# Where TensorE's two operands begin in SBUF, modulo 256 bytes, in a one-core hybrid layer

## The chip, the cores and the metric

The kernel runs on one core of one Trainium2 chip. The metric is the device time of one execution in microseconds. Three runs of the kernel before took 1450.31, 1451.68 and 1453.68 us; the median is 1451.68 us.

## The reference

One layer of an encoder trunk on x of 256 frames by 2048 channels, all in float32:

```
mod = silu(c) @ w_ada + b_ada                  # 2048 x 12288, split in six
h = rmsnorm(x, g0) * (1 + sc1) + sh1
q, k, v, r, lr, cb, cc, cx, ga, gb = split(h @ w_in)     # 2048 x 10256
o = gated linear attention(q, k, v, lr), by chunks of 64 frames, 4 heads
y_a = (rmsnorm(o) * silu(r)) @ w_out_gla       # 1024 x 2048
y_b = (cb * conv3(cc * cx)) @ w_out_conv       # 1024 x 2048
y = (sigmoid(ga) * y_a + sigmoid(gb) * y_b) @ w_o        # 2048 x 2048
x = x + g1 * rmsnorm(y, g_1)
h = rmsnorm(x, g_2) * (1 + sc2) + sh2
gate, up = split(h @ w_up)                     # 2048 x 11264
x = x + g2 * rmsnorm((gelu(conv3(gate)) * up) @ w_down, g_3)   # 5632 x 2048
```

## The kernel before

All weights, 362 MB, pass once from HBM through SBUF. Each product a @ w of float32 is made of three float32r matmuls: both operands are split in a rounded part (hi) and the rest (lo), and hi*hi, hi*lo and lo*hi are added up in PSUM. float32r is a 4-byte type that TensorE takes in one pass.

The work is a list, `stream`, of chunks. A chunk (class `Chunk`) is up to two blocks of 128 rows by 512 columns of one weight matrix. `pump` walks over the list: it issues the DMA of a chunk up to 13 places ahead (`LOOK_DMA`) into one of nine `raw` buffers, splits a chunk four places ahead (ScalarE casts `whi`, L283; VectorE subtracts and writes `wlo`, L292), and then has the matmuls of the chunk at hand issued. Between the chunks stand parts of the product with w_ada, which VectorE makes (`Ada` and `Gemv`, L424 to L472).

There are two kinds of matmul groups, and they put the operands the other way round:

- `Feat` (L339): the result has features on the partitions. The weights are stationary (128 columns of `whi` or `wlo`), and the activations move: 256 columns, one per frame, 258 in the first pair of groups of w_up. The activations are `h_hi` and `h_lo` (tile H), `yb` (tag B) for w_out_conv, `og` (tag g8) for w_out_gla, and `xs` (tile H again) for w_up.
- `Tok` (L394): the result has frames on the partitions. 128 frames of an activation are stationary, and 512 columns of the weights move. Stationary are H for k, v0 and v1 of w_in, `m_t` (tile H) for w_o, and `act` (tag g8) for w_down.

Each matmul has one weight load of its own (PEld). The load of the next matmul runs beside the matmul at hand.

All tiles come from one pool, which lays the tags one behind the other in the order of first use. By the allocation of this kernel, the tags that matter begin at these bytes of each partition: B at 31552, g8 at 47936 (four buffers of 8192), H at 85568 (36992 bytes), raw at 123392, whi at 168960, wlo at 185344. Modulo 256, B, all buffers of g8 and H are at 64; raw, whi and wlo are at 0. All steps inside the tiles that a matmul operand makes (a block of 128 or 512 columns, a row of H with 576 columns, 256 frames) are multiples of 256 bytes. So every `Feat` matmul reads its moving activations from 64 and its next stationary weights from 0, modulo 256, and every `Tok` matmul reads its moving weights from 0 and its next stationary activations from 64. The exceptions are small: L694 and L695, the projection for the forget gate, load 32 and 16 columns of a tile `t` that begin at 32 or at 160, beside 256 moving columns of H at 64.

The first stage makes the shift and scale for the first slice of two blocks of 128 channels (`SLICES[0]`). The product with w_ada for it is eight items `Ada(0, 0)` to `Ada(0, 7)`, each of two blocks of 128 rows by 512 columns, with two DMAs of 256 KB. VectorE adds up an item with two instructions (L472) into `acc_s`; the items in `ON_PE` are left to TensorE, which adds them up with small matmuls (L229, `sum_cols`). After the last item VectorE folds `acc_s` (L209, L211), TensorE finishes the sum over partitions (L217, `fold_cols`) into the same PSUM bank, and the first two blocks of H are made (`make_h`); with them the first `Feat` matmul starts.

Of the kernel before, what the change touches and what calls it, by code (L numbers as in the profile page):

```python
# [9 lines left out]
F32R = mybir.dt.float32r  # L10
# [5 lines left out]
P = 128  # L16
T = 256
D = 2048
KD = D // P
H = 4  # L20
# [7 lines left out]
TAU = 16.0  # L28
KT = 2
H_ROW = 576  # L30
NC = 512


# [7 lines left out]
G8 = 4  # L41
# [13 lines left out]
MID0, MID = 2, 4  # L55
SQ0, SQ1 = 3, 4
EARLY_G = [1, 0, 6, 13]
ON_PE = {(0, 5)}


@with_exitstack
def hybrid_layer(ctx, tc, x, c, w_ada, b_ada, norm_g, w_in, w_a2, b_a2, gla_norm_g,
# [7 lines left out]
    def sb(shape, tag, bufs=1, dt=F32):  # L70
        count[0] += 1
        return pool.tile(list(shape), dt, tag=tag, bufs=bufs, name=f"{tag}_{count[0]}")
# [5 lines left out]
    def sm_bank():  # L78
        count[0] += 1
        return psum.tile([P, 512], F32, tag="sm", bufs=2, name=f"sm_{count[0]}")  # L80

    def t2(cols=512):
        return sb([P, cols], "t2", T2)

    def t1(cols=T):
        return sb([P, cols], "t1", T1)
# [67 lines left out]
    def over(row, n):  # L154
        return row.rearrange("p (o t) -> p o t", o=1).to_broadcast([P, n, T])
# [15 lines left out]
    for s in range(2):  # L171
        for q in range(2):
            ps = mm_banks()
            for a in range(8):
                k = 8 * q + a
# [11 lines left out]
    gln = lambda i: p_col[:, 88 + i:89 + i]  # L187


    def moving():  # L190

        t = sb([P, KD * H_ROW + 32], "H", 1, F32R)[:, 0:KD * H_ROW].rearrange("p (k n) -> p k n", k=KD)
        return t[:, :, T:], t[:, :, 0:T]

    h_hi, h_lo = moving()
    mod1 = sb([P, 2, KD], "mod1")
    bmod1 = sb([P, 2, KD], "bmod1")
# [66 lines left out]
    class Chunk:  # L264
# [9 lines left out]
        def dma(self):  # L274
            g = self.g
            self.raw = sb([P, KT, NC], "raw", RAW_BUFS)[:, 0:self.n, :]
            r = g.row0 + self.k0 * P
            nc.sync.dma_start(
                self.raw, g.w[r:r + self.n * P, g.n0:g.n0 + NC].rearrange("(t p) n -> p t n", p=P))

        def split(self):
            self.hi = sb([P, KT, NC], "whi", SPLIT_BUFS, F32R)[:, 0:self.n, :]
            nc.scalar.copy(self.hi, self.raw)  # L283
            self.lo = sb([P, KT, NC], "wlo", SPLIT_BUFS, F32R)[:, 0:self.n, :]
            if pos[2] < first_w:
                first_lo.append(self.split_lo)
            else:
                self.split_lo()
# [154 lines left out]
    class Ada:  # L443
# [17 lines left out]
        def split(self):  # L461
            s = self.s
            for t in range(self.nk):
                if (s, self.i) in ON_PE:
                    break
# [14 lines left out]
        def mm(self):  # L480
            s = self.s
            if (s, self.i) in ON_PE:
                for t in range(self.nk):
# [56 lines left out]
    yb = {}  # L540
# [3 lines left out]
    qk, vt, sr, og = {}, {}, {}, {}  # L544
# [81 lines left out]
    def split_pair(hi, lo, src):  # L626
        copy = nc.scalar.copy(hi, src)
        nc.vector.tensor_sub(lo, src, f(hi))
        return copy.ins

    def tiles(t, n=2):
        return t.rearrange("p (a t) -> p a t", a=n)

    def post_cb(g):
        def post(j, v):
            if not yb:
                yb["t"] = sb([P, 2, 8, T], "B", 1, F32R)
            t = tiles(t2())
            nc.vector.tensor_mul(t, v, cc_t[g][:, 1, j:j + 2, :])
            k = 4 * g + j  # L640
            split_pair(yb["t"][:, 0, k:k + 2, :], yb["t"][:, 1, k:k + 2, :], t)
        return post
# [102 lines left out]
    def keys_values(h):  # L745

        kd = qk["t"][:, 1].rearrange("p (s d) -> p s d", s=2)
        kv = mm_banks()
        for c4 in range(4):
            s, half = c4 // 2, c4 % 2  # L750
            rows = slice(64 * half, 64 * half + 64)
            nc.tensor.matmul(kv[:, half, s * DV:(s + 1) * DV], kd[rows, s, h * DK:(h + 1) * DK],
                             vt["t"][rows, s, h * DV:(h + 1) * DV], start=True, stop=True)
        return kv

    def gla_heads():
        og["hi"] = sb([P, 8, T], "g8", G8, F32R)
        og["lo"] = sb([P, 8, T], "g8", G8, F32R)
        for h in range(H):
            S = sb([P, 4, DV], "c4", 2)  # L760
            kv = kvs.pop(h)
            nc.scalar.copy(S[:, 0, :], kv[:, 0, 0:DV])
            for c4 in range(1, 4):
                nc.vector.scalar_tensor_tensor(
                    S[:, c4, :], S[:, c4 - 1, :], dtot[:, 4 * c4 + h:4 * c4 + h + 1],
                    kv[:, c4 % 2, (c4 // 2) * DV:(c4 // 2 + 1) * DV], op0=ALU.mult, op1=ALU.add)
            yield
            yield
            po = sm_bank()
            qT = qk["t"][:, 0].rearrange("p (h t) -> p h t", h=4)[:, h, :]  # L770
            for dv in range(2):
                for c4 in range(4):
                    nc.tensor.matmul(po[:, dv * T + c4 * 64:dv * T + (c4 + 1) * 64],  # L773
                                     S[:, c4, dv * P:(dv + 1) * P], qT[:, c4 * 64:(c4 + 1) * 64],
                                     start=True, stop=True)
            sq = t2()
            nc.scalar.activation(sq, po, AF.Square)
            yield
            sum2 = t1()
            nc.vector.tensor_add(sum2, sq[:, 0:T], sq[:, T:2 * T])  # L780
            yield
            if h + 1 < H:
                kvs[h + 1] = keys_values(h + 1)
            pm = sm_bank()
            nc.tensor.matmul(pm[:, 0:T], ones, sum2, start=True, stop=True)
            yield
            rs = t1()
            nc.scalar.activation(rs, pm[:, 0:T], AF.Sqrt, scale=1.0 / DV, bias=eps)
            nc.vector.reciprocal(rs, rs)  # L789
            yield  # L790
            o = t2()
            ov = o.rearrange("p (a t) -> p a t", a=2)
            nc.vector.tensor_mul(ov, po.rearrange("p (a t) -> p a t", a=2), over(rs, 2))
            for dv in range(2):
                nc.vector.scalar_tensor_tensor(ov[:, dv, :], ov[:, dv, :], gln(dv), sr["t"][:, 0, 2 * h + dv, :],
                                               op0=ALU.mult, op1=ALU.mult)
            og["last"] = split_pair(og["hi"][:, 2 * h:2 * h + 2, :], og["lo"][:, 2 * h:2 * h + 2, :], ov)
            yield


    m_t, y_t = {}, {}
# [4 lines left out]
    def post_ya(g):  # L806
        def post(j, v):
            if not m_t:
                m_t["hi"], m_t["lo"] = moving()
            k = 4 * g + j  # L810
            t = tiles(t2())
            nc.vector.tensor_mul(t, v, ga_t["t"][:, k:k + 2, :])
            nc.vector.tensor_add(t, t, gb_t["t"][:, k:k + 2, :])
            split_pair(m_t["hi"][:, k:k + 2, 0:T], m_t["lo"][:, k:k + 2, :], t)
        return post
# [299 lines left out]
    run_all(bg)  # L1115

    bg = gla_heads()
    pump(stream.index(gla_to) + 1 - pos[2], each=step_bg)
    run_all(bg)
# [22 lines left out]
    with tc.high_priority():  # L1142
        xs["hi"], xs["lo"] = moving()
        nc.vector.tensor_copy(xs["hi"][:, :, T], sh2)
        nc.vector.tensor_sub(xs["hi"][:, :, T + 1], sh2, f(xs["hi"][:, :, T]))
        for q in range(4):
            n = slice(512 * q, 512 * (q + 1))
            for s in range(2):
                def x1():
                    return nc.vector.scalar_tensor_tensor(  # L1150
                        xin["t"][:, s, n], y_t["t"][:, s, n], r1[:, s:s + 1], xin["t"][:, s, n],
                        op0=ALU.mult, op1=ALU.add).ins
                if len(mid) == 3:
                    with tc.issue_after(mid[2]):
                        x1()
                else:
                    ins = x1()
                    if s == 1:
                        mid.append(ins)
            for k in range(4 * q, 4 * q + 4, 2):  # L1160
                ps = sm_bank()
                for a in range(2):
                    for s in range(2):
                        nc.tensor.transpose(ps[:, a * T + s * P:a * T + (s + 1) * P],  # L1164
                                            xin["t"][:, s, (k + a) * P:(k + a + 1) * P], ident)
                for a in range(2):
                    sc, v = s2[:, k + a:k + a + 1], ps[:, a * T:(a + 1) * T]
                    hi = xs["hi"][:, k + a, 0:T]
                    mid_act.append(nc.scalar.mul(hi, v, sc).ins)
                    nc.vector.scalar_tensor_tensor(xs["lo"][:, k + a, :], v, sc, f(hi),  # L1170
                                                   op0=ALU.mult, op1=ALU.subtract)
# [63 lines left out]
```

## Time and profile before

| | us |
|---|---|
| median of the runs shown | 1451.68 |
| the profiled execution's own time | 1453.29 |
| span of its trace, first to last instruction | 1451.5 |
| TensorE matmuls busy (PE) | 1425.8 (98%) |
| weight loads busy (PEld) | 1336.3 (92%) |
| VectorE busy (DVE) | 1036.6 (71%) |
| ScalarE busy (ACT) | 792.9 (55%) |

The span stands beside the execution's own time: 1.8 us lie around it. A matmul's duration in the trace runs from its start to the end of its drain, so it overlaps with the next ones; what counts for the time is the distance from one start to the next, which a row of the chain of waits gives as its time divided by its count.

### The profile page before, as it was taken

Reading aid. Unit: us, or ns where it says so; the run is one execution under the profiler, and the core shown is the slowest. Engines: PE = TensorE matmul, PEld = TensorE weight load, DVE = VectorE, ACT = ScalarE, POOL = GpSimd, SP = SyncE. Lnnn points to the kernel's source line nnn. Section 1 sums busy time; section 2 is a strip of 40 time slices with the busy share of each in tenths; the row PEclk is TensorE's granted clock in tenths of the full one; section 3 lists DMA queues with packets and bytes.
Section 4 is the critical chain, followed back from the end, with each engine's and each line's share of the span. In section 5 each row is a group of like instructions: output and inputs, shape, how many; then the busy total and the mean of one; then the engine's idle time right before and its main releaser. Section 6 shows DMA issues by size and latency. Waiting matters only on the chain.

```text
span 1451.5 us, 25558 instructions
## 1 busy us (share of the span) xinstructions
PE 1425.8 (98%) x10385; PEld 1336.3 (92%) x10385; DVE 1036.6 (71%) x1153; ACT 792.9 (55%) x952; POOL 7.1 (0%) x28
## 2 busy tenths in 40 slices
PE   6999999999999999999999999999999999999997
PEld 6999999899999999887999998789999988999986
DVE  6887878889988877975897666656666644555554
ACT  5788777689554655444764444344444433444443
POOL 0000000000000000000000000000000000000000
PEclk9999999999999999999999999999999999999999
DMA  9999989989988778886568777677776666666651
GB/s 353 366 339 310 375 286 360 328 288 331 372 285 280 245 251 317 304 299 183 151 199 264 238 234 235 231 239 236 230 228 204 200 188 190 187 184 185 186 174 59
DMA packets 178095, 366.97 MB, mean 253 GB/s; under 512 B 14026, under 2 KB 26648, under 8 KB 177209
## 3 DMA queue, kind: packets, MB, share of 16 engines
q1 hardware_dynamic: 176857, 362.17, 75.4%
q0 software_dynamic: 544, 2.11, 0.4%
q8 instruction: 81, 1.33, 0.4%
q10 hardware_dynamic: 576, 1.05, 0.2%
q14 instruction: 37, 0.30, 0.1%
HBM read 363.18 MB, written 2.11 MB: 252 GB/s over the span
## 4 chain that ended last, share of the span: by engine, by line
PE 93%; DVE 3%; DMA 2%; ACT 1%; issue 1%; SPq 0%; DVEq 0%; ACTq 0%
PE mm L339 63%; PE mm L394 28%; DMA raw<-in_w_ada_dram 2%; DMA XF<-in_x_dram 1%; DVE wlo L292 0%; DVE c L432 0%; DMA raw<-in_w_in_dram 0%; PE sm L1164 0%; SPq L458 0%; ACT whi L283 0%; DVE t L789 0%; PE sm L773 0%; DVE fold L211 0%; DVE c L472 0%; PE sm L217 0%
## 5 line engine op out<-in xcount | busy, mean ns | idle before, releaser
L283 ACT CAST whi<-raw 128x1024 fp32r<-128x1024 f32 (+1 forms) x503 | 512.6, 1024 | 525.3 <-PE mm L339 280.4
L292 DVE TENSOR_TENSOR wlo<-raw,whi 128x1024 fp32r<-128x1024 f32 (+1 forms) x503 | 595.4, 1191 | 285.5 <-ACT whi L283 275.7
L339 PE MATMUL mm<-H,whi 128*128 128x256 f32 (+1 forms) x4992 | 649.3, 281 | 1.6 <-ACT H L254 1.2
L339 PEld LDWEIGHTS mm<-H,whi 128*128 128x128 f32 x4992 | 616.1, 189 | 3.9 <-ACT H L254 1.3
L339 PE MATMUL mm<-H,wlo 128*128 128x256 f32 (+1 forms) x2496 | 350.2, 280 | 0.0
L339 PEld LDWEIGHTS mm<-H,wlo 128*128 128x128 f32 x2496 | 318.5, 188 | 0.0
L394 PE MATMUL mm<-whi,g 128*128 128x512 f32 x704 | 181.5, 395 | 0.0
L394 PEld LDWEIGHTS mm<-whi,g 128*128 128x128 f32 x704 | 131.9, 188 | 31.7
L432 DVE SCALAR_TENSOR_TENSOR c<-raw,sil,c 128x1024 f32<-128x1024 f32 x90 | 115.2, 1280 | 35.7 <-DMA raw<-in_w_ada_dram 35.6
L394 PE MATMUL mm<-whi,H 128*128 128x512 f32 x448 | 118.5, 396 | 0.0
L394 PEld LDWEIGHTS mm<-whi,H 128*128 128x128 f32 x448 | 83.5, 188 | 19.6
L394 PE MATMUL mm<-wlo,g 128*128 128x512 f32 x352 | 99.3, 395 | 0.0
L394 PEld LDWEIGHTS mm<-wlo,g 128*128 128x128 f32 x352 | 66.1, 188 | 16.0
L472 DVE SCALAR_TENSOR_TENSOR c<-raw,sil,c 128x768 f32<-128x768 f32 (+2 forms) x73 | 78.6, 1077 | 2.0 <-DMA raw<-in_w_ada_dram 1.4
L394 PE MATMUL mm<-wlo,H 128*128 128x512 f32 x224 | 65.7, 395 | 0.0
L432 DVE SCALAR_TENSOR_TENSOR cb<-raw,sil,cb 128x1024 f32<-128x1024 f32 x30 | 38.5, 1284 | 24.7 <-DMA raw<-in_w_ada_dram 24.7
L394 PEld LDWEIGHTS mm<-wlo,H 128*128 128x128 f32 x224 | 42.1, 188 | 10.2
L982 DVE SCALAR_TENSOR_TENSOR t<-mm,fcol,t 128x255 f32<-128x255 f32 x80 | 38.4, 480 | 1.2
L339 PE MATMUL mm<-B,whi 128*128 128x256 f32 x256 | 33.5, 282 | 0.0
L339 PE MATMUL mm<-g,whi 128*128 128x256 f32 x256 | 32.8, 280 | 0.0
L339 PEld LDWEIGHTS mm<-B,whi 128*128 128x128 f32 x256 | 31.4, 188 | 1.4 <-ACT t L712 0.8
L339 PEld LDWEIGHTS mm<-g,whi 128*128 128x128 f32 x256 | 31.3, 188 | 0.0
(193 smaller groups left out, 687.1 us busy)
## 6 DMA issues: line engine op xcount, KB each, us to landing
raw<-in_w_up_dram SPq DMA_DIRECT2D x176, 512.0 KB, 4.3
raw<-in_w_ada_dram SPq DMA_DIRECT2D x160, 512.0 KB, 5.2
raw<-in_w_in_dram SPq DMA_DIRECT2D x145, 512.0 KB, 5.8
raw<-in_w_down_dram SPq DMA_DIRECT2D x88, 512.0 KB, 3.8
raw<-in_w_o_dram SPq DMA_DIRECT2D x32, 512.0 KB, 5.6
raw<-in_w_ada_dram SPq DMA_DIRECT2D x32, 384.0 KB, 6.1
raw<-in_w_out_conv_dram SPq DMA_DIRECT2D x16, 512.0 KB, 6.1
raw<-in_w_out_gla_dram SPq DMA_DIRECT2D x16, 512.0 KB, 5.4
```

The lines of the kernel that those rows point to most:

```text
L283: nc.scalar.copy(self.hi, self.raw)
L292: nc.vector.tensor_sub(self.lo, self.raw, f(self.hi))
L339: nc.tensor.matmul(dst[:, 0:cols], w[:, t, j * P:(j + 1) * P], m(ch.k0 + t, cols), start=first_in_bank and t == 0 and i == 0, stop=end and ...
L394: nc.tensor.matmul(self.out[s], m(c.k0 + t, T)[:, s * P:(s + 1) * P], w[:, t, :], start=first and t == 0 and i == 0, stop=end and t == c.n ...
L432: nc.vector.scalar_tensor_tensor(a, self.raw, sil[:, self.k:self.k + 1], a, op0=ALU.mult, op1=ALU.add)
L472: nc.vector.scalar_tensor_tensor(a, raw, sc, a, op0=ALU.mult, op1=ALU.add)
L982: nc.vector.scalar_tensor_tensor(dst[:, a, i:], v[:, a, 0:T - i], w(2 - i, a), dst[:, a, i:], op0=ALU.mult, op1=ALU.add)
```

## The change

Three things are done.

- A tile for moving activations gets 64 more elements, and the activations begin 32 elements (`OPPOSITE`, 128 bytes) inside it: H where it is `h` and `xs`, `yb`, and both parts of `og`. H has 48 elements (`H_PAD`) behind its rows instead of 32. Where H holds `m_t`, the stationary activations of w_o, it begins at the tile's beginning, as `act` does in its unchanged tile.
- Since B grows by 256 bytes, each of the four buffers of g8 by 256, and H by 64, all tiles behind H (raw, c4, whi, wlo, A, cb and the small ones) move up by 1344 bytes, which is 64 modulo 256. The tiles ahead of them keep their places modulo 256.
- `ON_PE` names the last item of the first slice, (0, 7), in place of (0, 5).

```diff
+H_PAD = 48
+OPPOSITE = 32
-ON_PE = {(0, 5)}
+ON_PE = {(0, 7)}
-    def moving():
-        t = sb([P, KD * H_ROW + 32], "H", 1, F32R)[:, 0:KD * H_ROW].rearrange("p (k n) -> p k n", k=KD)
+    def parted(shape, tag, bufs=1):
+        n = shape[0] * shape[1]
+        t = sb([P, n + 64], tag, bufs, F32R)[:, OPPOSITE:OPPOSITE + n]
+        return t.rearrange("p (k n) -> p k n", k=shape[0])
+    def moving(at=OPPOSITE):
+        t = sb([P, KD * H_ROW + H_PAD], "H", 1, F32R)[:, at:at + KD * H_ROW]
+        t = t.rearrange("p (k n) -> p k n", k=KD)
         return t[:, :, T:], t[:, :, 0:T]
-                yb["t"] = sb([P, 2, 8, T], "B", 1, F32R)
+                yb["t"] = parted([16, T], "B").rearrange("p (a k) n -> p a k n", a=2)
-        og["hi"] = sb([P, 8, T], "g8", G8, F32R)
-        og["lo"] = sb([P, 8, T], "g8", G8, F32R)
+        og["hi"] = parted([8, T], "g8", G8)
+        og["lo"] = parted([8, T], "g8", G8)
-                m_t["hi"], m_t["lo"] = moving()
+                m_t["hi"], m_t["lo"] = moving(0)
```

## Rows read from the trace of the kernel before

**Rows 1.** The page: busy time by engine; then the chain's shares by engine and line.
```profile
PE 1425.8 (98%) x10385; PEld 1336.3 (92%) x10385; DVE 1036.6 (71%) x1153; ACT 792.9 (55%) x952; POOL 7.1 (0%) x28
...
PE 93%; DVE 3%; DMA 2%; ACT 1%; issue 1%; SPq 0%; DVEq 0%; ACTq 0%
```

**Rows 2.** The page's groups: line, engine, out<-in, count | busy us, mean ns | idle before.
```profile
L339 PE MATMUL mm<-H,whi 128*128 128x256 f32 (+1 forms) x4992 | 649.3, 281 | 1.6 <-ACT H L254 1.2
...
L339 PE MATMUL mm<-H,wlo 128*128 128x256 f32 (+1 forms) x2496 | 350.2, 280 | 0.0
...
L394 PE MATMUL mm<-whi,g 128*128 128x512 f32 x704 | 181.5, 395 | 0.0
...
L394 PE MATMUL mm<-whi,H 128*128 128x512 f32 x448 | 118.5, 396 | 0.0
...
L394 PE MATMUL mm<-wlo,g 128*128 128x512 f32 x352 | 99.3, 395 | 0.0
...
L394 PE MATMUL mm<-wlo,H 128*128 128x512 f32 x224 | 65.7, 395 | 0.0
...
L339 PE MATMUL mm<-B,whi 128*128 128x256 f32 x256 | 33.5, 282 | 0.0
L339 PE MATMUL mm<-g,whi 128*128 128x256 f32 x256 | 32.8, 280 | 0.0
```

**Rows 3.** The chain of waits, whole span: start us, us, what, xcount.
```profile
969.44 144.16 PE mm L339 x1224
...
1150.72 89.60 PE mm L394 x384
```

**Rows 4.** The chain of waits from 743 to 764 us.
```profile
742.92 20.13 PE mm L339 x177
```

**Rows 5.** Stretches, L339 alone: stretch, us, PE and PEld busy (count), clock, DMA, GB/s.
```profile
748.00:760.00 12.00, 12.00 (x108) 12.00 (x107) 1.00 0.67 186
800.00:812.00 12.00, 12.00 (x104) 12.00 (x103) 1.00 0.78 247
```

**Rows 6.** Order of time, end of the last Tok group: start us, us, engine.
```profile
1442.58 0.19 PEld L394 LDWEIGHTS mm<-wlo,g 128*128 128x128 f32 x1
...
1442.81 0.40 PE L394 MATMUL mm<-wlo,g 128*128 128x512 f32 x1
```

**Rows 7.** Order of time, eight matmuls of the forget gate's projection.
```profile
398.05 0.28 PE L694 MATMUL sm<-H,t 128*32 128x256 f32 x1
398.05 0.09 PEld L695 LDWEIGHTS sm<-H,t 128*16 128x16 f32 x1
398.17 0.28 PE L695 MATMUL sm<-H,t 128*16 128x256 f32 x1
...
398.29 0.28 PE L694 MATMUL sm<-H,t 128*32 128x256 f32 x1
...
398.87 0.28 PE L695 MATMUL sm<-H,t 128*16 128x256 f32 x1
```

**Rows 8.** Order of time, the first slice; idle before in brackets.
```profile
14.42 3.90 DVE L472 SCALAR_TENSOR_TENSOR c<-raw,sil,c 128x512 f32<-128x512 f32 x5 [0.15 <-DMA raw<-in_w_ada_dram]
...
19.21 3.12 DVE L472 SCALAR_TENSOR_TENSOR c<-raw,sil,c 128x512 f32<-128x512 f32 x4 [0.88 <-DMA raw<-in_w_ada_dram]
...
19.94 1.87 PEld L229 LDWEIGHTS sm<-sil,raw 128*128 128x128 f32 x16
...
22.36 0.71 DVE L209 STREAM_TRANSPOSE raw<-c 128x512 f32<-128x512 f32 x1
...
23.84 0.25 PE L217 MATMUL sm<-fold,sel 128*32 128x4 f32 x8 [1.95 <-DVE fold L211]
```

**Rows 9.** Stretches, all engines: us, PE, PEld, DVE, ACT, POOL, clock, DMA, GB/s.
```profile
25.00:120.00 95.00, 94.59 (x701) 90.33 (x702) 80.53 (x85) 75.58 (x88) 0.00 (x0) 0.97 1.00 359
120.00:208.00 88.00, 87.92 (x673) 83.89 (x671) 70.09 (x65) 66.32 (x74) 0.00 (x0) 1.00 0.93 328
```

**Rows 10.** DMA from 0 to 30 us: GB/s in 40 slices of 0.75 us.
```profile
GB/s 0 0 11 153 208 448 404 404 448 382 386 337 361 386 343 381 272 274 321 351 377 362 376 384 382 386 392 400 377 407 410 397 378 401 412 396 411 383 394 400
```

## The prediction

> **What bounds the kernel now.** I read the page's busy times and the shares of the chain of waits first. TensorE is busy for 98% of the span, and 93% of the chain is TensorE [rows 1]; the two places that issue matmuls in bulk are L339 (`Feat`) and L394 (`Tok`). So the time is set by the distance between starts of matmuls, times their count, and by a few stalls. The groups give the counts [rows 2]: for L339, 4992 + 2496 with H, 256 with B and 256 with g, 8000 in all (two groups of 128 with wlo, too small for the page, are left out of the sum); for L394, 704 + 448 + 352 + 224 = 1728. The distances come from the chain in order of time [rows 3]: 144.16 us / 1224 = 117.8 ns for a `Feat` matmul of 256 columns, 89.60 / 384 = 233.3 ns for a `Tok` matmul of 512. At 2.4 GHz, one column a cycle, 256 columns would be 106.7 ns and 512 would be 213.3. So each `Feat` matmul takes 11.1 ns and each `Tok` matmul 20.0 ns more than its columns, with the granted clock at 1.00. 8000 x 11.1 + 1728 x 20.0 is 123 us: that is the whole amount the change can reach for.
>
> The row that tells most is an exception. From 742.92 us on, 177 matmuls of L339 took 20.13 us, which is 113.7 ns each [rows 4]. Two stretches of 12 us show the same shapes from the same places in SBUF, both at clock 1.00, with 108 matmuls in the one and 104 in the other [rows 5]. Nothing that the code says differs between the two stretches. So the excess over the columns is not a constant of the type: the same pair of reads, of moving columns and of next weights, can settle in a slow rhythm and in a quicker one. That speaks for two streams that get in each other's way depending on how they lie to one another, and the change alters exactly that, in bytes.
>
> **The change part by part.**
>
> *Places.* B, g8 and H were at 64 and the weights at 0, modulo 256. Growth of 256 + 4 x 256 + 64 = 1344 bytes puts the weights at 64; `h`, `xs`, `yb` and `og` go to 64 + 128 = 192, `m_t` and `act` stay at 64. So the distance of moving from stationary goes from 64 to 128 in `Feat`, and from 192 to 0 in `Tok` for w_o and w_down. k, v0 and v1 keep H as stationary operand and get 128. These three are 3 x 16 x 6 = 288 matmuls, so 1440 of `Tok` get the distance 0. No instruction is added or taken away by this.
>
> *Feat.* The trace doesn't show a distance of 128. The price is bounded by the nearest rows. Below: a matmul can't start before its weights are in, and loads that have nothing to wait for come every (1.87 - 0.19) / 15 = 112 ns (16 loads at L229, beside matmuls of one column [rows 8]; a load takes 0.19 [rows 6]), so at most 5.8 ns are gained. Above: in the gate's projection the loaded columns begin at 32 or 160 while the moving ones begin at 64; the distances there are 32 and 160, and the step across a distance of 160 reads 0.12 us, from 398.17 to 398.29 [rows 7], so up to 2.2 ns lost. I take the quicker rhythm, 113.7 ns: it is the only other value at which bulk matmuls of this form are seen to settle, and it lies near the lower bound. 177 of the 8000 have it already, so 7823 x 4.1 ns = 32.1 us. Not all of it can be had: from 25 to 120 us the DMA engines are busy all the time at 359 GB/s [rows 9], and a quicker TensorE would wait for weights there; its 701 matmuls (of both kinds) are at most 701 x 4.1 ns = 2.9 us. From 120 us on the share is 0.93, which leaves room for a demand that is 3.5% faster (4.1 / 117.8); VectorE is busy 70.09 of 88 us there. Left: 29.2 us. What is late next is the weights' split on VectorE and ScalarE, but not yet.
>
> *Tok.* Distance 0 isn't shown in a steady run either. A load is through after about 112 ns [rows 8], the first half of a matmul of 512, and the excess goes nearly with the columns (11.1 and 20.0), as if the half without a load were as slow. I take no gain. Bounds: 20.0 ns gained, 1440 x 20.0 = 28.8 us, and 2.2 ns lost, as above, 3.2 us.
>
> *The last item on TensorE.* VectorE idles 0.88 us before four instructions of 0.78 us (3.12 / 4) for items 6 and 7; then comes the fold, 22.36 to 23.84, and TensorE's part at 23.84 [rows 8]. With (0, 7) on TensorE, VectorE adds item 5 from 18.33 (14.42 + 3.90), if its data are there, to 19.89, item 6 to 21.45, and the fold ends at 22.93: 0.9 us sooner. TensorE's 16 loads for item 7 take 1.87 us, and VectorE didn't wait for item 7's data at 20.77; so they are done by 22.7, ahead of the fold. If item 5's data come as late as item 6's, 19.2, only 0.1 us is won. The buffer of item 5 is freed sooner and that of item 7 about 0.4 us later, in SP's queue, which at that time has w_in's chunks to issue; the stretch after it is bound by DMA, so between 0 and 0.9 us is kept. I take 0.9.
>
> *The move of raw.* The weights' DMAs now write to 64 modulo 256 where they wrote to 0. The first two big transfers, x into XF, go to a tile at 32 modulo 256, and while they run 404 to 448 GB/s are moved [rows 10], more than in any later slice. So a start off 256 costs nothing here; price 0. The Trainium skill, "DMA: Bandwidth & Descriptors", section "How a descriptor splits into AXI transactions", says that a transfer is cut at multiples of 256 bytes, and that one that starts off them needs an extra transaction. Carried over to the writing side, which it doesn't say, a row of 2048 bytes would take nine in place of eight; that is an estimate of +12.5% DMA time from that page, some 12 us from 25 to 120 us alone. The trace of XF doesn't bear it out.
>
> *Sum.* 1453.3 (own time of the profiled execution) - 29.2 - 0.9 = 1423.2. The median of the runs is 1.6 us below that execution, so 1422.
>
> **The rivals.**
>
> *No change.* The excess belongs to the moving stream alone. For it: the last matmul of all, with no load beside it (the last load began at 1442.58 and took 0.19, the matmul began at 1442.81), took 0.40 us [rows 6], as long as the mean of 395 to 396 ns of its kind with a load beside it [rows 2]. And eight matmuls beside loads of 16 or 32 columns, an eighth to a fourth of the usual, came every (398.87 - 398.05) / 7 = 117 ns [rows 7], as those beside full loads. Against it: 113.7 ns exists. Then only the 0.9 us remains: 1452.4, or 1451 by the median. If the pool placed the tiles otherwise than I worked out, it would end here too. The Trainium skill, "TensorE: Matmul & The Clock Gate", Part 2, states the rule behind it: TensorE has two independent read ports in SBUF, one for the moving operand and one for weight loads, so loading the next weights takes nothing from the running matmul. By that rule, no placement matters; rows 6 and 7 agree with it, rows 4 doesn't.
>
> *Both kinds lose most of the excess.* `Feat` comes down to its loads, 112 ns: 7823 x 5.8 = 45.4 us; `Tok` to its columns: 28.8 us. With 0.9: 1378, by the median 1377. For it: the loads in rows 8. Against: nothing shows a `Tok` matmul near 213 ns, and DMA would be the bound up to 398 us.
>
> *Slower: the new distance is a worse one.* The step across 160 is 0.12 us [rows 7], and 128 is nearer to 160 than to the others that the trace shows (0 in single steps, 32, 64, 192). If all `Feat` matmuls went to 120 ns, 8000 x 2.2 = 17.6 us, less 0.9: 1470, by the median 1468. It decides from the first w_in chunk on, everywhere. Against it: the steps around it are shorter by as much, so that the mean of the eight is 117. A second way to this side is raw's new place: if the writes slowed by a tenth, an assumption, the 95 us at DMA share 1.00 would grow by 9.5 and the 88 us at 0.93 by 3% or 2.6 [rows 9]; less 0.9 that is 1464.5, by the median 1463. Rows 10 speak against it. The DMA rule above would end here.
>
> **How the numbers follow.** The quicker rhythm in `Feat`: 0.44. Both kinds: 0.13. No change: 0.24. Slower: 0.13 by the distance, 0.06 by DMA. Faster by over 0.2% (2.9 us, about what a measurement of this kernel can tell from no change) is 0.57, within it 0.24, slower 0.19. The range must hold the quicker rhythm and no change and reach a little to both sides: 1385 to 1460 leaves out most of the case with both kinds and the worst of the slower one. The likeliest case has its own range, 1405 to 1438, from 112 ns everywhere to half of the matmuls at 113.7.
>
> **What would show it.** Right: in the chain, L339 rows at 113 to 114 ns a matmul over long stretches, with the clock at 1.00; L394 rows still near 233; the first L339 matmul at about 24.4 us in place of 25.3; DMA share near 1.00 up to 400 us. Wrong: L339 at 117.8 (no change), at 119 or more (worse distance), L394 well under 230 (the excess is a matter of place for both), or new idle time of ScalarE's casts that DMA ended (raw's new place costs).

## The result, and the profile after

The changed kernel takes 1455.6 us (median of 20 runs, 1453.4 to 1458.3) beside 1451.9 us for the kernel before (20 runs, 1445.2 to 1454.0). The ratio is 1.0031, 95% interval 1.0022 to 1.0040: slower by 0.31%, some 4.5 us. The prediction was 1422 us, faster. It was wrong in its direction.

All line numbers after the first edits are 9 higher: L339 is L348, L394 is L403, L229 is L238, L209 is L218, L217 is L226. The page of the changed kernel, busy times, the chain's shares by engine, and three groups that answer to [rows 1, 2]:

```profile
PE 1426.1 (98%) x10385; PEld 1345.9 (93%) x10385; DVE 1036.2 (71%) x1153; ACT 792.6 (55%) x952; POOL 7.1 (0%) x28
...
PE 90%; DMA 5%; DVE 3%; issue 1%; ACT 0%; SPq 0%; DVEq 0%; ACTq 0%
...
L348 PE MATMUL mm<-H,whi 128*128 128x256 f32 (+1 forms) x4992 | 655.6, 283 | 1.6 <-ACT H L263 1.2
...
L403 PE MATMUL mm<-whi,g 128*128 128x512 f32 x704 | 177.0, 389 | 0.0
...
L403 PE MATMUL mm<-whi,H 128*128 128x512 f32 x448 | 116.8, 392 | 0.0
```

TensorE is still what bounds the kernel, with the same count of matmuls and the same busy time. That the chain goes through DMA for 5% where it was 2% costs TensorE little: its longest wait of that kind, for VectorE in the attention, grew from 0.4 to 1.3 us. But the two kinds moved against each other: the duration of one `Feat` matmul went from 281 to 283 ns, of one `Tok` matmul of w_down from 395 to 389. The distances from start to start are in the chain of waits of the changed kernel (start us, us, what, count):

```profile
603.12 73.47 PE mm L403 x324
...
719.79 162.48 PE mm L348 x1368
...
969.76 146.88 PE mm L348 x1224
...
1154.03 87.05 PE mm L403 x384
```

146.88 / 1224 = 120.0 ns, where it was 117.8 [rows 3], and 162.48 / 1368 = 118.8 ns. 73.47 / 324 = 226.8 ns (w_o) and 87.05 / 384 = 226.7 ns (w_down), where it was 233.3 [rows 3]. Over all steady matmuls of the trace (the distance from one start to the next, stalls left out) `Feat` went from 117.7 to 119.2 ns and `Tok` of w_o and w_down from 233.3 to 226.8; k, v0 and v1, which got distance 128, went from 233.3 to 232.5. So:

- `Feat`: 8256 matmuls (the 8000 of [rows 2] and two groups of 128 with wlo) x 1.5 ns = +12.4 us.
- `Tok` of w_o and w_down: 1440 x -6.5 ns = -9.4 us; k and v: 288 x -0.8 ns = -0.2 us.
- The first `Feat` matmul starts at 26.56 us where it was 25.34: +1.2 us.

The sum is +4.0 us; the medians differ by 3.7. Of its terms the last is the least certain, since the start varies: the ten profiled kernels that leave raw at 0 modulo 256 start `Feat` between 25.34 and 26.17 us, the four that move it by 64 between 25.78 and 26.64. The late start shows in the order of time of the first slice (idle before in brackets), which answers to [rows 8]:

```profile
14.68 7.08 DVE L481 SCALAR_TENSOR_TENSOR c<-raw,sil,c 128x512 f32<-128x512 f32 x9 [0.19 <-DMA raw<-in_w_ada_dram]
...
21.56 1.95 PE L238 MATMUL sm<-sil,raw 128*128 128x1 f32 x16 [0.26 <-DMA raw<-in_w_ada_dram]
...
23.54 0.71 DVE L218 STREAM_TRANSPOSE raw<-c 128x512 f32<-128x512 f32 x1 [1.77 <-PE sm L238]
...
25.03 0.29 PE L226 MATMUL sm<-fold,sel 128*32 128x4 f32 x8 [1.52 <-DVE fold L220]
...
26.56 0.58 PE L348 MATMUL mm<-H,whi 128*128 128x256 f32 x1 [1.25 <-ACT H L263]
```

VectorE is through with its seven items at 21.76 (14.68 + 7.08), but its fold begins at 23.54 only and waits 1.77 us for TensorE's sum (L238). The fold transposes into a tile of the tag raw, and of the nine buffers of this tag it gets, by the order of the code, the one in which item 7 lies. So the fold can't begin before TensorE has read item 7.

### The profile page after: what moved, and what is told of

Its sections match the earlier page's. It is cut to its first block, busy times and chain, and to the rows that moved or that the text cites. A ratio compares the mean times of both kernels' runs of the same rounds, so it can differ in the third digit from the quotient of the medians.

```text
span 1453.1 us, 25560 instructions
## 1 busy us (share of the span) xinstructions
PE 1426.1 (98%) x10385; PEld 1345.9 (93%) x10385; DVE 1036.2 (71%) x1153; ACT 792.6 (55%) x952; POOL 7.1 (0%) x28
## 4 chain that ended last, share of the span: by engine, by line
PE 90%; DMA 5%; DVE 3%; issue 1%; ACT 0%; SPq 0%; DVEq 0%; ACTq 0%
PE mm L348 62%; PE mm L403 27%; DMA raw<-in_w_ada_dram 4%; DVE wlo L301 1%; DVE c L441 1%; DMA XF<-in_x_dram 1%; DVE t L798 0%; DMA raw<-in_w_in_dram 0%; PE sm L782 0%; DVE fold L220 0%; DVE raw L218 0%; PE sm L1173 0%; DVE XF L1159 0%; PE sm L226 0%; PE mm L761 0%
## 5 line engine op out<-in xcount | busy, mean ns | idle before, releaser
L348 PE MATMUL mm<-H,whi 128*128 128x256 f32 (+1 forms) x4992 | 655.6, 283 | 1.6 <-ACT H L263 1.2
L348 PEld LDWEIGHTS mm<-H,whi 128*128 128x128 f32 x4992 | 621.8, 189 | 4.0 <-ACT H L263 1.3
L348 PE MATMUL mm<-H,wlo 128*128 128x256 f32 (+1 forms) x2496 | 353.8, 283 | 0.0
L348 PEld LDWEIGHTS mm<-H,wlo 128*128 128x128 f32 x2496 | 321.2, 189 | 0.0
L403 PE MATMUL mm<-whi,g 128*128 128x512 f32 x704 | 177.0, 389 | 0.0
L403 PEld LDWEIGHTS mm<-whi,g 128*128 128x128 f32 x704 | 131.9, 188 | 27.2
L403 PE MATMUL mm<-whi,H 128*128 128x512 f32 x448 | 116.8, 392 | 0.0
L403 PEld LDWEIGHTS mm<-whi,H 128*128 128x128 f32 x448 | 83.5, 188 | 17.7
L403 PE MATMUL mm<-wlo,g 128*128 128x512 f32 x352 | 97.0, 389 | 0.0
L403 PEld LDWEIGHTS mm<-wlo,g 128*128 128x128 f32 x352 | 66.1, 188 | 13.7
L403 PE MATMUL mm<-wlo,H 128*128 128x512 f32 x224 | 64.9, 392 | 0.0
L403 PEld LDWEIGHTS mm<-wlo,H 128*128 128x128 f32 x224 | 42.1, 188 | 9.2
L348 PE MATMUL mm<-B,whi 128*128 128x256 f32 x256 | 33.8, 284 | 0.0
L348 PE MATMUL mm<-g,whi 128*128 128x256 f32 x256 | 33.1, 282 | 0.0
L348 PEld LDWEIGHTS mm<-B,whi 128*128 128x128 f32 x256 | 31.6, 188 | 1.3 <-ACT t L721 0.8
L348 PEld LDWEIGHTS mm<-g,whi 128*128 128x128 f32 x256 | 31.5, 188 | 0.0
```

The source lines that it names most:

```text
L348: nc.tensor.matmul(dst[:, 0:cols], w[:, t, j * P:(j + 1) * P], m(ch.k0 + t, cols), start=first_in_bank and t == 0 and i == 0, stop=end and ...
L403: nc.tensor.matmul(self.out[s], m(c.k0 + t, T)[:, s * P:(s + 1) * P], w[:, t, :], start=first and t == 0 and i == 0, stop=end and t == c.n ...
```

## The experiments

The theories, with the numbers that the expectations use: (1) the distance between the places of a matmul's two operands, modulo 256 bytes, sets its rhythm; (2) the place of the moving operand alone sets it; (3) places have no effect, and something else made the difference. All kernels of this section but raw64, pe_only, places_only and shift64 keep raw, whi and wlo at 0 modulo 256 and TensorE's item at (0, 5), so that only distances differ from the kernel before. In the kernels of the scan and those built like it, L339 is L349 and L394 is L404. "Distance" is always moving less next stationary, modulo 256.

### A scan of distances

Against the changed kernel, cut:

```diff
-H_PAD = 48
-OPPOSITE = 32
+H_PAD = 96                                        # weights at 0 again
+H_AT, YB_AT, OG_AT, XS_AT = 48, 56, 8, 24         # scan_a
+M_AT, ACT_AT = 40, 32
-ON_PE = {(0, 7)}
+ON_PE = {(0, 5)}
-    def moving(at=OPPOSITE):
+    def moving(at):
-    h_hi, h_lo = moving()
+    h_hi, h_lo = moving(H_AT)      # and likewise yb, og, m_t, xs, and act by parted(..., ACT_AT)
```

scan_b has 32, 40, 52, 44 and 24, 56; scan_c 36, 4, 60, 12 and 8, 44; scan_d 12, 28, 20, 32 and 52, 48.

> Weights and raw are at 0 modulo 256 as in the kernel before; each activation has a place of its own, so that moving minus next stationary, modulo 256, is 0 for h, 32 for yb, 96 for og, 160 for xs (all Feat), 0 for k and v, 32 for w_o, 64 for w_down (all Tok). The look is at the distance between starts of matmuls in each group. Theory 1, the distance of the two reads that run side by side sets the rhythm: the groups differ; Feat has 117.8 ns at 64 and 119.2 at 128 already, so og between (118.5), xs about 120, h and yb under 117 (single steps at 0 and 32 read 115 to 116 before); Tok near 227 ns at 0 and between 227 and 233 at 32 and 64. Theory 2, the place of the moving operand alone sets it: Tok moves from 0 modulo 256 here in all three groups, as in the kernel before, so all three stay at 233.3 ns. Theory 3, the excess belongs to the moving stream whatever the places: all Feat groups 117.8, all Tok groups 233.3.

> As the first scan, with distances 192 for h, 224 for yb, 16 for og, 240 for xs (Feat), 64 for k and v, 96 for w_o, 224 for w_down (Tok). Theory 1: groups differ; by what is known so far og at 16 under 117 ns, h at 192 about 120, yb and xs between them; Tok at 96 near 231 ns, at 224 between 227 and 233. Theory 2: all Tok at 233.3 ns. Theory 3: Feat 117.8, Tok 233.3 everywhere.

> As the first scan, with distances 208 for h, 80 for yb, 48 for og, 112 for xs (Feat), 48 for k and v, 160 for w_o, 16 for w_down (Tok). Theory 1: Feat rises from under 117 ns at 48 over 118 at 80 to 119 at 112; 208 near 120; Tok at 16 near 227 ns, at 160 near 233. Theory 2: all Tok at 233.3 ns. Theory 3: Feat 117.8, Tok 233.3 everywhere.

> Edit: as the kernels of the scan (weights and raw at 0 modulo 256, ON_PE = {(0, 5)}), with h and xs changed over: moving less next stationary, modulo 256, is 112 for h (it was 192 and 208), 176 for yb, 144 for og, 192 for xs (it was 112 and 240); in Tok 144 for k and v, 240 for w_o, 0 for w_down. Theory 1 (the distance of the two reads sets the rhythm, whichever tile and stage): h near 113.5 ns with some more in the stretch up to 120 us that is bound by DMA, xs near 114.5, w_down near 227, yb, og and w_o not known; 1415 to 1425 us. Rival (the quick rhythm is a matter of the stage or of the load on VectorE and DMA there, and xs at 192 or h at 112 don't have it): one of the two stays at 117 ns or more, 1432 us or more.

Measured, one run each: scan_a 1455.9, scan_b 1442.2, scan_c 1436.1 us beside 1452.0 for the kernel before, scan_d 1431.8 beside 1452.5 (28 runs). scan_d misses the 1415 to 1425 us of its expectation: h at 112 is quick, but xs at 192 takes 116.5 ns and not 114.5. The means of the steady distances from start to start, in ns, by distance of the operands in bytes (with those of the kernels before, after and mixed, below). Most of them come from one execution of one kernel:

| `Feat`, moving | ns by distance |
|---|---|
| h | 0: 119.9; 64: 117.7; 104: 124.9 (two rhythms); 112: 113.7; 128: 119.0; 192: 114.5; 208: 119.0 |
| xs | 64: 117.7; 112: 113.9; 120: 120.7; 128: 119.5; 160: 118.4; 192: 116.5; 240: 117.2 |
| yb | 32: 117.1; 64: 117.8; 80: 119.7; 116: 121.8; 128: 118.8; 176: 119.2; 224: 118.3 |
| og | 16: 118.7; 48: 118.4; 64: 117.8; 96: 120.0; 108: 120.0; 128: 118.7; 144: 118.0 |

| `Tok`, stationary | ns by distance |
|---|---|
| m_t, act | 0: 226.8; 16: 228.1; 32: 233.3; 64: 228.9; 96: 233.3; 160: 234.3; 192: 233.3; 224: 233.3; 240: 233.3 |
| h (k, v) | 0: 227.3; 48: 232.3; 64: 229.5; 128: 232.5; 144: 233.9; 192: 233.3 |

The same 1224 and 384 matmuls of [rows 3] in the chain of waits of scan_a (xs at 160, act at 64), then scan_c (xs at 112, act at 16), then scan_d (xs at 192, act at 0):

```profile
972.24 145.25 PE mm L349 x1224
...
1155.30 87.92 PE mm L404 x384
```

```profile
967.29 138.76 PE mm L349 x1224
...
1141.84 87.69 PE mm L404 x384
```

```profile
952.20 144.16 PE mm L349 x1224
...
1133.49 87.08 PE mm L404 x384
```

118.7, 113.4 and 117.8 ns; 229.0, 228.4 and 226.8 ns. Theory 3 falls. Theory 2 falls by the `Tok` rows: the moving weights lie at 0 in all four kernels, and the time goes from 226.8 to 234.3 with the place of the stationary operand. Theory 1 holds in that changing h and xs over (scan_d) took the quick rhythm along with distance 112. In these four kernels the weights always lie at 0, so the place of the activations alone would explain the rows as well; shift64, below, decides between the two. What no theory had is the form: there is no slope, but a few distances that are good, and 192 is in between, because at that distance the matmuls spend part of the time in a rhythm of 113 to 114 ns and part at 117 to 119. Neither end of the step that the change made, 64 to 128, was a good one for `Feat`.

### The rest of the change, one part at a time

raw64 is the kernel before with only the destination of the weights' DMAs moved (and the accumulators c4 that lie behind it); pe_only is the kernel before with only the other item; places_only is the changed kernel with the old item. The cuts leave out the lines that only keep the padding.

```diff
 # raw64: 64 bytes of padding ahead of the first raw tile, 192 ahead of the first whi tile
+    nc.gpsimd.memset(sb([P, 16], "pad0"), 0.0)
+                padded_w.append(sb([P, 48], "pad1"))
 # pe_only
-ON_PE = {(0, 5)}
+ON_PE = {(0, 7)}
 # places_only, against the changed kernel
-ON_PE = {(0, 7)}
+ON_PE = {(0, 5)}
```

> Edit: the kernel before, with 64 bytes of padding ahead of the raw buffers and 192 bytes ahead of whi. So raw begins at 64 modulo 256 as in the changed kernel, and every distance between the operands of a matmul stays as before. Theory 1 (the writes of the weights' DMAs to rows that begin at 64 modulo 256 are slower, and the distances set the rhythm of TensorE): the 256 KB transfers of w_ada at the start land about 0.75 us apart in place of 0.68, the first chunks of w_in 1.35 us apart in place of 1.28; the first Feat matmul starts 0.3 to 0.6 us later; up to 400 us, where the DMA engines are nearly always busy, some more waits; in all +0.5 to +3 us. Feat stays at 117.7 ns, Tok at 233.3 ns. Rival (the later landings in the changed kernel come from the item given to TensorE, or from chance): landings as before, time within 0.1% of before. Rival (raw's place is what slowed Feat to 119.2 ns): Feat goes to 119 ns here, +10 us or more.

> Edit: the kernel before, with ON_PE = {(0, 7)} and nothing else. Theory 1 (the fold's scratch tile takes the raw buffer of item 7 and so waits for TensorE's sum of that item): the fold's transposition waits for L229, as in the changed kernel; the first Feat matmul starts 0.2 to 0.8 us later than before; +0.1 to +0.8 us in all, at the edge of what can be measured. Rival (the prediction's term: VectorE has less to do ahead of the fold, and nothing else holds it): the first Feat matmul starts up to 0.9 us sooner, up to -0.9 us in all.

> Edit: the changed kernel, with ON_PE = {(0, 5)} as before, so that only the places differ from the kernel before. Theory 1: what places make of the time is all of the change but the item on TensorE: Feat at 119.2 ns (+12 us over 8256 matmuls), Tok at distance 0 at 226.8 ns (-9.4 us over 1440), slower writes; so 1452.5 to 1456, 0.1 to 0.8 us under the changed kernel. Rival (the item on TensorE is what makes the changed kernel slower): at or under the time of before, 1452 or less.

Measured, against 1452.5 us (28 runs): raw64 1452.2 us, ratio 1.0007 (0.9994 to 1.0021); pe_only 1452.1, ratio 1.0000 (0.9987 to 1.0013); places_only 1455.6, ratio 1.0024 (1.0013 to 1.0036).

So the places are nearly all of the loss, and the item on TensorE is neither a gain nor a loss that can be told: in pe_only the fold waits 1.14 us for L229, and the first `Feat` matmul starts at 25.49 us, 0.15 later than before. The move of raw does slow the transfers at the start. The DMA view from 15 to 27 us, first of the kernel before, then of raw64:

```profile
DMA packets 3563, 4.68 MB, mean 390 GB/s; under 512 B 211, under 2 KB 2539, under 8 KB 3563
```

```profile
DMA packets 3357, 4.40 MB, mean 367 GB/s; under 512 B 200, under 2 KB 2352, under 8 KB 3357
```

390 became 367 GB/s in a stretch in which the DMA engines are always busy. By this rate alone the effect is 1 to 7%: the ten kernels with raw at 0 have 372 to 391 GB/s there, the four with raw at 64 have 362 to 368. The landings tell it more sharply, and alike in all four: 1.35 to 1.37 us apart for the first chunks of w_in in place of 1.28, and 0.75 us for 256 KB of w_ada in place of 0.68. The first `Feat` matmul of raw64 starts at 25.78, 0.44 later, which is within the spread of the kernels with raw at 0. Beyond the start, the interval of raw64, from 0.9 us less to 3.1 us more, leaves open what it costs.

The Trainium skill, "DMA: Bandwidth & Descriptors", section "How a descriptor splits into AXI transactions", has, for reads, one more transaction for a row of 1 or 2 KB that starts off a multiple of 256 bytes; worked out from that page, an estimate, it would be 12.5% for rows of 2 KB and 25% for those of 1 KB if the transactions are counted, and 3% and 6% by the beats of 32 bytes that the page counts as well. It doesn't say whether this holds for writes. The traces, for writes, agree in the sign and lie between, with 5% and 10%.

One more thing is seen in pe_only, whose operands lie as before. Its profiled execution, the fastest of its twelve, has a span of 1443.8 us where the kernel before has 1451.5. Its chain of waits has these two rows, and the kernel before has the two below for the same matmuls:

```profile
129.24 54.15 PE mm L339 x476
...
205.35 60.72 PE mm L339 x534
```

```profile
130.27 56.26 PE mm L339 x476
...
208.50 63.09 PE mm L339 x534
```

That is 113.8 and 113.7 ns, where the kernel before took 118.2 and 118.1. The excursions to the quick rhythm, of which [rows 4] is one, come and go from run to run at distance 64. These two groups alone are 4.5 us, so the excursions can make much of the spread of the runs of before.

### Feat alone and Tok alone

The rest of these two kernels is as in the scan:

```diff
 # feat128: distance 128 in Feat as in the change, 192 in Tok as before
+H_AT, YB_AT, OG_AT, XS_AT = 16, 16, 16, 16
+M_AT, ACT_AT = 0, 0
 # tok0: distance 64 in Feat as before, 0 in Tok of w_o and w_down as in the change
+H_AT, YB_AT, OG_AT, XS_AT = 0, 0, 0, 0
+M_AT, ACT_AT = 48, 48
```

> Edit: weights and raw at 0 modulo 256 as before, ON_PE = {(0, 5)}; the moving activations of Feat begin at 128 (distance 128, as in the changed kernel), the stationary ones of w_o and w_down stay at 64 (distance 192, as before). Theory 1 (by distance): Feat 119.2 ns, so 8256 x 1.5 = 12.4 us over before, about 1464.5; Tok for w_o and w_down 233.3 ns. Rival (raw or the weights at 64 were needed for the slower rhythm): Feat at 117.7 ns, 1452.5 us.

> Edit: weights and raw at 0, ON_PE = {(0, 5)}, Feat's moving activations at 64 (distance 64) as before; the stationary activations of w_o and w_down begin at 0 (distance 0, as in the changed kernel). Theory 1 (by distance): Feat 117.5 ns, Tok 226.8 ns, so 1440 x 6.5 = 9.4 us under before, about 1443. Rival (the prediction's term: no gain in Tok; what the changed kernel shows there comes from somewhere else): 1452.5 us.

Measured, against 1453.3 us (9 runs): feat128 1463.7 us, ratio 1.0080 (1.0060 to 1.0101); tok0 1442.8 us, ratio 0.9937 (0.9915 to 0.9959). The chain of waits of feat128, then of tok0:

```profile
974.59 146.88 PE mm L349 x1224
...
1158.87 89.60 PE mm L404 x384
```

```profile
963.04 144.16 PE mm L349 x1224
...
1144.33 87.07 PE mm L404 x384
```

Each part comes alone as it came in the change: 120.0 ns beside 233.3, and 117.8 beside 226.7. By the ratios that is +11.6 us (8.7 to 14.7) and -9.2 us (-6.0 to -12.4), together +2.4; with the 0.9 us by which places_only starts `Feat` later (26.22 for 25.34) +3.3, where places_only measured +3.5 (1.9 to 5.2). So the parts add up to the whole, within intervals of some 3 us either way.

### The good distances together, and the same 64 bytes further on

```diff
 # best: weights and raw at 0
+H_AT, YB_AT, OG_AT, XS_AT = 12, 12, 12, 12
+M_AT, ACT_AT = 48, 48
 # shift64: weights and raw at 64 (H_PAD = 48), every distance the same
+H_AT, YB_AT, OG_AT, XS_AT = 28, 28, 28, 28
+M_AT, ACT_AT = 0, 0
```

> Edit: weights and raw at 0, ON_PE = {(0, 5)}; all moving activations of Feat at 112 (distance 112), the stationary ones of w_o and w_down at 0 (distance 0; k and v come to 144). Theory 1 (by distance): Feat 113.5 ns after the first stage, yb and og too, Tok of w_o and w_down 226.8: 8256 x 4.1 = 34 us, of which 2 to 4 stay with the stretch up to 120 us that waits for DMA, and 9.4 us; 1408 to 1414 us. Rival (DMA or the split of the weights becomes the bound once TensorE is quicker): rhythm at 113.5 but new waits for whi or wlo, 1418 us or more.

> Edit: all distances of the kernel with 112 and 0 (Feat 112, w_o and w_down 0, k and v 144), but everything lies 64 bytes further on: weights and raw at 64, moving activations at 176, stationary ones at 64, modulo 256. Theory 1 (the distance alone counts): Feat near 113.5 ns and Tok near 227 ns as there; time within 3 us of it, with up to 1 us more from raw at 64. Rival (the places themselves count too, for instance whether an operand begins at a multiple of 128 or 256): Feat at 116 ns or more, 1425 us or more.

Measured: best 1417.9 us (1415.3 to 1418.1), ratio 0.9757 (0.9736 to 0.9777) to the kernel before, 32 to 38 us less; it beats both kernels. shift64 1420.0 us in one run, within the 3 us that its expectation allowed. The chain of waits of best, then of shift64:

```profile
950.01 138.76 PE mm L349 x1224
...
1124.56 87.07 PE mm L404 x384
```

```profile
952.41 138.76 PE mm L349 x1224
...
1126.95 87.07 PE mm L404 x384
```

113.4 and 226.7 ns in both: the distance counts, not the place, for this shift by 64 bytes, and yb and og too are at 113.7 to 114.3 with distance 112. best is 4 to 10 us behind its expectation, and there the rival has its share. By the starts of the same matmuls, best is 12.1 us ahead at 467 us of the time before, 12.6 at 762 and 35.1 at 1423: in between it gains next to nothing. PE's groups in best from 458 to 628 us, and below them the same two groups of the kernel before from 470 to 640 us, show one cause:

```profile
L349 PE MATMUL mm<-g,wlo 128*128 128x256 f32 x128 | 17.7, 280 | 1.3 <-DVE wlo L302 1.3
...
L795 PE MATMUL sm<-t,ones 128*128 128x256 f32 x6 | 2.1, 426 | 2.6 <-DVE t L790 2.6
```

```profile
L339 PE MATMUL mm<-g,wlo 128*128 128x256 f32 x128 | 17.7, 279 | 0.0
...
L785 PE MATMUL sm<-t,ones 128*128 128x256 f32 x6 | 2.1, 426 | 0.4 <-DVE t L780 0.4
```

VectorE, which has the split of the weights, the product with w_ada and the attention to do there, comes late as soon as TensorE is quicker: in these two groups TensorE waits for it 3.5 us more. The other cause is the rhythm itself. The same 384 matmuls at the start of w_up, in the chain of waits of the kernel before, then of best:

```profile
718.31 44.74 PE mm L339 x384
```

```profile
705.68 44.80 PE mm L349 x384
```

There is no gain in them. The second part of these matmuls, from [rows 4], had the quick rhythm in the kernel before already. The first part belongs to the pair of groups in which two of three matmuls have 258 columns; by starts in the trace they take 118.8 ns in best and 118.7 in the kernel before, with the clock at 1.00. So the distance 112 is good for 256 columns, and isn't for this mixture with 258.

### Own operand or the one loaded beside it, and how narrow 112 is

Cut; the other places that read `act` follow:

```diff
+H_AT, YB_AT, OG_AT, XS_AT = 10, 13, 11, 14        # distances 104, 116, 108, 120
-                act[g] = parted([8, T], "g8", ACT_AT, G8).rearrange("p (a k) n -> p a k n", a=2)
+                t = sb([P, 8 * T + 64], "g8", G8, F32R)[:, ACT_AT:ACT_AT + 8 * T + 16]
+                n = 4 * T
+                act[g] = [t[:, i:i + n].rearrange("p (k n) -> p k n", k=4) for i in (0, n + 16)]
```

> Edit: as the kernel with Feat at 112 and w_o and w_down at 0, but the distances of Feat are 104 for h, 116 for yb, 108 for og, 120 for xs, and in w_down act_lo lies 64 bytes further on than act_hi. So a matmul with act_hi has distance 0 to its own stationary operand and, in the passes that alternate, 192 to the one that is loaded beside it; a matmul with act_lo has 192 to its own and 0 to the one loaded beside it; in the third pass both are 0. Theory 1 (the matmul's read and the read of the next weights beside it): a matmul whose next load is act_lo takes about 233 ns, one whose next is act_hi about 227. Rival (its own stationary operand counts): the act_lo matmuls take 233, the act_hi ones 227. Second rival (neither by itself: a pair shares one rhythm): both kinds of matmul take the same in the alternating passes. For Feat: if the quick rhythm at 112 is a wide place, 104 to 120 stay below 115 ns, and the time is 1418 to 1424 us; if it is a narrow one, h and xs go to 118 to 120 ns, 7300 x 5 = 36 us, about 1455 us.

Measured: 1483.6 us in one run, beside 1450.5 for the kernel before: 112 is a narrow place. The time is 28 us above even the expectation for a narrow one. Of the neighbours, 104, 116 and 120 are worse than any other distance that was tried, with 124.9, 121.8 and 120.7 ns, and 108, with 120.0, is as bad as 96 and 0. The chain of waits of mixed:

```profile
136.47 57.59 PE mm L349 x476
...
216.48 69.61 PE mm L349 x534
...
993.59 148.24 PE mm L349 x1224
...
1179.64 87.96 PE mm L404 x384
```

121.0 ns (h at 104), then 130.4 ns for the next group at the same distance, and 121.1 (xs at 120). In the group of 534 the trace has steps of 122 and 138 ns in turn, all the way: one distance has more than one rhythm, and each can last for a whole group.

In w_down, by starts in the trace, none of the three accounts in the expectation holds as stated. In the 82 chunks with alternating passes, these matmuls come in fours, with mean steps of 226.4 (act_hi), 235.4 (act_lo), 231.7 (act_hi) and 227.2 ns (act_lo). Those of the third pass, with both distances 0, take 226.9. The two act_lo have the same distances, 192 to their own operand and 0 to the one loaded beside them, and yet one takes 235 and the other 227; the two act_hi differ by 5 ns in the same way. So neither the own operand nor the one loaded beside it gives the time of a matmul by itself: several matmuls share a pattern. That is so in the kernel before too, where all have 192 and the steps alternate between 231 and 235 ns. The four take 920.7 ns together, half way between four at distance 0 (907) and four at 192 (933). Whose read is held up isn't shown by this run.

## Why the prediction was wrong

**What bounds the kernel** was right: TensorE's distance from start to start. Nearly all of the differences measured here are that distance or a wait that it uncovers; the later start of `Feat`, up to 1.2 us, is the exception.

**Places** was right: the times follow the distances that were worked out, and the distances are what counts (feat128, tok0, shift64).

**Feat** is the step that failed: "I take the quicker rhythm, 113.7 ns". It was priced at -29.2 us and measured +12.4 by the trace, +11.6 by feat128. The quicker rhythm exists, and the excess does go with how the two operands lie. But the price of distance 128 was taken from the best rhythm seen at distance 64, as if another distance had to lead there. No row showed 128, so the bounds were all there was, -5.8 to +2.2 ns a matmul; the measured +1.5 is near the upper one. That bound came from a step across distance 160 [rows 7], and it spoke for slower. Nor was it as good as it looked: in bulk, 160 gives 118.4 ns (scan_a), while a single step of 0.12 us is rounded to 10 ns. The lower bound held: the 112 ns between loads stayed the floor, and no group came below 113.3.

**Tok** was mis-sized: 0 was taken, -9.4 us measured (1440 x 6.5 ns), inside its bounds of -28.8 and +3.2. The step that failed is "I take no gain" for a distance that no row showed. Its reason, that the half of a matmul without a load beside it is as slow, took the 112 ns between loads for the length of a load, which is 0.19 us in [rows 6], most of the 233 ns of a matmul. The last matmul of all, with no load beside it, can't bear it out either: with the same distance of 192 it took 397 ns in the kernel before (0.40 us in [rows 6]) and 390 in feat128, and at 64 (scan_a) and 16 (scan_c), which are nearly alike in bulk, 388 and 397. Whether a matmul without a load beside it is slow stays open; that place matters is shown by tok0.

**The last item on TensorE** failed as well: -0.9 us was forecast, and the fold then waits for L238. Its working looked at VectorE's and TensorE's queues, but not at the buffer that the fold's scratch tile gets. By pe_only it is worth 0 within 2 us.

**The move of raw** was priced at 0 by [rows 10]. That row was of XF, whose rows are 8 KB long, and it could not tell for rows of 1 and 2 KB. With these the landings lie 10% and 5% further apart (raw64). What that costs in the whole stays open: raw64's interval holds 0 and 3 us. In the rival built on it, 88 us at a share of 0.93 would grow by 2.3% with writes slower by a tenth, which is 2.0 us and not 2.6.

**The rivals.** "Slower: the new distance is a worse one" came about, with 119.2 ns for the 120 it was priced at and with the gain in `Tok` against it; without that gain it would be feat128's 1464, near the 1468 of that rival. Two signs that the prediction had named as wrong are in the changed kernel: L348 at 119 ns or more, and L403 well under 230. "No change" falls with the scan. "Both kinds lose most of the excess" did not come about; best goes a part of the way, by other distances, with 113.4 and 226.7 ns: 4.4 of the 11.1 ns and 6.6 of the 20.0. The rule behind "no change", in the Trainium skill, "TensorE: Matmul & The Clock Gate", Part 2, is that loads of the next weights take no read bandwidth of SBUF from the running matmul. No run here shows whether they do. The conclusion that the prediction drew from it, that no placement matters, the measurements contradict, with 226.7 and 233.3 ns for matmuls that differ only in the place of the stationary operand.

What stays open is the mechanism: why 112 is good and 104 and 120 are bad for `Feat`, why 258 columns don't gain by it, while `Tok` is best at 0. That 256 bytes are the period was taken for granted and not tested. And a mean that comes from one execution may be one of several rhythms of its distance.

## What to carry to other kernels

Where TensorE is the bound and the type is float32r, the places of the two operands modulo 256 bytes are a tuning parameter worth up to 10% of a matmul here (113.4 to 124.9 ns) and 2.4% of the kernel (best). They are to be scanned on the chip, for each shape of matmul and more finely than in steps of 16 bytes, with several tiles at different distances in one kernel, and never reckoned by a rule such as "far apart is good". A rhythm seen for a while in a trace tells that it exists, not which placement leads to it. Where work is handed from one engine to another, look at which buffer the next step takes before a gain is counted.

## What was not expected of the hardware

- One `Feat` matmul of 256 columns takes 113.4 to 124.9 ns on average by the distance of its operands, and 130.4 in one stretch, all at a granted clock of 0.99 to 1.00 (the level of 2.4 GHz); one `Tok` matmul of 512 columns takes 226.7 to 234.3.
- Four bytes are enough: 112 gives 113.8 ns for yb and 113.9 for og, 116 gives 121.8 for yb and 108 gives 120.0 for og (best, mixed).
- The good distance belongs to a shape: where two of three matmuls have 258 columns in place of 256, they take 118.8 ns at 112 and 118.7 at 64 (best, before).
- At 64, 104 and 192 the rhythm isn't unique: at 64 whole groups of 500 matmuls run at 113.7 in one execution and at 118.1 in another, with the same placement.
- Writing rows of 1 KB to 64 modulo 256 in place of 0 spaces the landings of 256 KB by 0.75 us in place of 0.68 (raw64).
